# Fewer unread products in front, unread products between the sums of the norm, another price list for the order, and three late rows in flight in place of two

## The chip, the cores and the metric

The kernel runs on one core of one Trainium2 chip, as one program with one launch. The time is the device time of one execution in microseconds (us), and the figure for a kernel is the median over several executions.

## The reference

One layer of a diffusion backbone over 512 latent tokens and 256 context tokens, width 1024, all in float32:

```python
mod   = silu(c) @ w_ada + b_ada          # 6 vectors of 1024: shift, scale, gate, twice
mod_c = silu(c_ctx) @ w_ada + b_ada
h  = rms_norm(x, g_norm1) * (1 + sc1) + sh1
hc = rms_norm(ctx, g_norm1) * (1 + csc1) + csh1
aq, ak, av, dq, dk, dv, dz, da, db, ga, gd = split_cols(h @ w_in)      # the same for hc
y_attn = window_ctx_attention(q_a, k_a, v_a, k_ac, v_ac, attn_sink)    # 8 heads, window 128
o_dc, s_cf, s_cb = bidir_delta(context ...)      # gated delta rule, chunks of 64, both directions
o_dl, _, _       = bidir_delta(latent ..., s_cf, s_cb)
y = sigmoid(ga) * (y_attn @ w_br_attn) + sigmoid(gd) * (y_d @ w_br_dn)
x_new = x + gt1 * (y @ w_out)
x_new = x_new + gt2 * (square(relu(hm @ w_mlp1)) @ w_mlp2)   # hm: second norm, with sh2, sc2
```

## The kernel before

Activations lie transposed, features on the 128 partitions and tokens along the free dimension. A float32 product that must be exact is made of three products of rounded float32 (`mm3`: upper by upper, upper by lower, lower by upper; lines 331, 333 and 335). A product of plain float32 shows in the trace as two matmul instructions.

**The front.** Constants are set, `NONES` products of `ones` by `ones` (line 230) run on TensorE, and nobody reads them. The DMA queue of SyncE (SP) loads x, the context and sixteen halves of the first two sixths of `w_ada`. `norm_x` squares x in four pieces (ScalarE, line 402), folds each piece (VectorE, line 405) and sums over the partitions with one plain float32 product per piece (line 406); `Ln` and `Exp` make the factor `rx`. `ada(kt)` (line 249) and `columns(kt, ...)` (lines 267 to 282) make scale and shift of one block of 128 features; `features(kt)` (lines 339 to 341) makes the normalized, modulated block, and `early_x` and `early_c` multiply it with three early weight tiles. Two more groups of unread products stand in the front: eight after the first `columns` (line 276, `NWAIT`) and eleven more behind later ones (line 434, `WARM`). All other products of the layer follow these.

**The late modulation.** The other four sixths of `w_ada` are no matmuls: `late_mod` loads 32 rows of 512 KB each and sums each on VectorE (line 511). The load of a row waits for the sum of the row `NROWS` before it:

```python
d = nc.sync.dma_start(out=wa.ap, in_=I["wada2"][grp, j])
if len(sums) >= NROWS:
    tie(d.ins, sums[-NROWS], sync)
r = V.scalar_tensor_tensor(wa.ap, wa.ap, 0.5, scr_[0].ap, ...)
```

The first 16 of them stand beside the stage in which the delta rule's inverse is combined (`combine`, lines 993 to 1017), the intra-chunk matrices are made (`half_products`, line 894; lines 1395 to 1408) and the latent scan begins (`chain_step`, small products, line 1243). Products of the branch and gate projections fill TensorE there (`run_fill`, line 1148).

**The order.** The program is written once in a plain order. Then `arrange` gives every engine and the SP queue one fixed order: `Lists.run` is a list scheduler. It keeps a clock for TensorE, VectorE, ScalarE, GpSimd and SP, has a price for every instruction (`Step.cost`, how long it holds its engine and when its result is there), and takes on each engine the ready instruction with the lowest rank. The rank is the place in the written order, moved by `SHIFTS`: entries (engine or -1 for all, first place, end place, how many places to move). So a changed price or shift changes no instruction, only the order in which an engine takes them. DMA issues have their place in the SP order in the same way.

Of the kernel before, what the change touches and what calls it, by code (L numbers as in the profile page):

```python
# [26 lines left out]
LEAD = 0  # L27
ATT = 32
NHALF = 3
NONES, NWAIT = 30, 8  # L30
AHEAD = 2
LATES = 3, 3
HPAUSE = 2
# [3 lines left out]
STICK = 50  # L37
NSKIP = 2
WARM = (0, 3, 3, 3, 2, 0, 0, 0)
NROWS = 2  # L40
ND1 = 3
NGD = 5
P = 128
# [8 lines left out]
HC = CH // 2  # L52
# [65 lines left out]
def tile_layer(ctx: ExitStack, tc: tile.TileContext, I: dict, out: bass.AP, dbg=None):  # L118
    nc = tc.nc
    V, A, G, PE = nc.vector, nc.scalar, nc.gpsimd, nc.tensor  # L120
# [17 lines left out]
    banks = Arena(lambda o, n: psum[:, o:o + n], 512, 8)  # L138
# [55 lines left out]
    ones = mats.tile([P, P], F32, name="ones")  # L194
# [33 lines left out]
    wb_ = banks.get(512, True)  # L228
# [166 lines left out]

    def norm_x():
        ss = bank()
        for i in range(4):
            b = alloc(1024)
            src = xs_[:, i * 1024:(i + 1) * 1024]  # L400
            n = 512 if i == 3 else 1024
            A.activation(b[:, :n], src[:, :n], AF.Square)
            if i == 3:
                V.tensor_tensor(b[:, n:], src[:, n:], src[:, n:], op=ALU.mult)
            V.tensor_tensor(b[:, :512], b[:, :512], b[:, 512:], op=ALU.add)
            PE.matmul(ss.ap, ones, b[:, :512], start=(i == 0), stop=(i == 3))
            b.free()
        act(rx, ss.ap, AF.Ln, bias=epsc, scale=1.0 / D)
        ss.free()
        return act(rx, rx, AF.Exp, scale=-0.5)  # L410
# [177 lines left out]
    own = [slice(0, 64), slice(64, 128)]  # L588
# [1163 lines left out]
class Step:  # L1752
# [39 lines left out]
    def cost(self):  # L1792

        n = self.cols
        if self.kind == "InstMatmult":
            if self.dtype.endswith("32r"):
                return (226 if n == 512 else max(60, 7 + .44 * n)), n * .44 + 175
            if self.dtype.endswith("16"):
                return 96, 240
            if self.whole:  # L1800
                return (110, 280) if self.ins.is_transpose else (max(62, 1.72 * n), max(62, 1.72 * n) + 170)
            return (142, 300) if self.tile[0] == P else (30 if self.tile[1] > HC else 19, 220)
        if self.kind == "InstStreamTranspose":
            return 1950, 2090
        if self.eng == "DVE":
            own = 67 + 1.04 * n + 60 * self.psum if n > 8 else 100
            return own, own + 85
        if self.eng == "Activation":
            own = 1290 if "Load" in self.kind else max(195, 36 + .893 * n) + 20 * self.psum
            return own, own + 130  # L1810
        return 550, 560
# [69 lines left out]
class Lists:  # L1881
# [27 lines left out]
    def run(self, rank):  # L1909

        n, after, gang, eng = self.n, self.after, self.gang, self.eng
        left, ready = list(self.left), [0.] * len(self.left)
        wait = [len(m) for m in self.members]
        free, links = [0., 0., 0., 0., 750.], [0., 0., 0., 0., 3200.]
        coming, here, out = [[] for _ in free], [[] for _ in free], []
        flight, whole, cold = [], True, False
        words, asked, begun, last = 0, {n: 0. for n in range(3)}, [0.] * n, 0.
        push, pop = heapq.heappush, heapq.heappop
        note = [SEEN[e] for e in self.ENGINES]

        def go(k):
            if k >= n:
                for x in after[k]:
                    ready[x] = max(ready[x], ready[k])
                    left[x] -= 1
                    if not left[x]:
                        go(x)
            elif gang[k] is None:
                push(coming[eng[k]], (ready[k], rank[k], k))
            else:  # L1930
                g = gang[k]
                wait[g] -= 1
                if not wait[g]:
                    t = max(ready[x] for x in self.members[g])
                    for x in self.members[g]:
                        push(coming[0], (t, rank[self.members[g][0]], x))

        for k in [k for k, m in enumerate(left) if not m]:
            go(k)
        for _ in range(n):  # L1940
            t, e = min((free[e] if here[e] else max(free[e], coming[e][0][0]), e) for e in range(5) if here[e] or coming[e])
            mine, come = here[e], coming[e]
            while come and come[0][0] <= t:
                push(mine, pop(come)[1:])
            k = mine[0][1]
            if e == 0 and self.whole[k] != whole:
                same = min((x for x in mine if self.whole[x[1]] == whole), default=None)
                if same and same[0] <= mine[0][0] + STICK:
                    k = same[1]
                    mine.remove(same)  # L1950
                    heapq.heapify(mine)
                else:
                    pop(mine)
            else:
                pop(mine)
            out.append(k)
            if self.dma[k]:
                if e == 4:
                    if len(flight) >= 8:
                        t = max(t, flight[-8])  # L1960
                    links[e] = end = max(t + (2400 if self.bytes[k] > 100000 else 1600), links[e]) + self.bytes[k] / 422
                    flight.append(end)
                    free[e] = t + 400
                else:
                    links[e] = end = max(t + 2400, links[e]) + self.bytes[k] / 159
                    free[e] = t + 900
            else:
                own, lag = self.cost[k]
                if e == 0:
                    words, had = words + self.words[k], words  # L1970
                    block = int(words / 256 + .63)
                    if block > int(had / 256 + .63):
                        asked[block] = max(t + 1100, links[4] - 500) + 1250
                    t = max(t, asked.get(int(had / 256 - .54), 0))
                    if self.whole[k] != whole:
                        t += 92 if whole else 130
                        cold = whole = self.whole[k]
                    elif cold and whole and self.wide[k]:
                        t, cold = t + 100, False
                end = t + lag  # L1980
                free[e] = t + own
            begun[k], last = t, max(last, end)
            for x in after[k]:
                if x >= n:
                    at = end + 40
                elif eng[x] == e and not self.dma[k]:
                    at = free[e] if e == 0 else end + 10
                else:
                    at = end + note[eng[x]]
                if at > ready[x]:  # L1990
                    ready[x] = at
                left[x] -= 1
                if not left[x]:
                    go(x)
        return out, begun, last


SHIFTS = (
# [12 lines left out]
)  # L2011


# [120 lines left out]
```

## Time and profile before

| | us |
|---|---|
| median of 3 executions | 871.31 |
| lowest and highest | 870.93, 871.32 |
| the profiled execution: its time | 871.5 |
| its span in the profile | 869.7 |

The span runs from the first instruction to the last; 1.8 us of the profiled execution lie around it. PE is TensorE's matmuls, PEld its weight loads, DVE is VectorE, ACT is ScalarE, POOL is GpSimd, SPq the DMA issues of SyncE. A matmul's end is modelled and reaches into the next one, so the sum of durations of a group is more than the time that it takes. "L406" is line 406 of the kernel before.

### The profile page before, as it was taken

To read this page: it belongs to the slowest core of one execution; us is meant where nothing else is said; L and a number is where in the kernel's file an instruction comes from. 1 tells how busy PE (TensorE), PEld (TensorE's weight loads), DVE (VectorE), ACT (ScalarE), POOL (GpSimd) and SP (SyncE) were. 2 spreads that over 40 slices of the span, in tenths; PEclk is the share of its full clock that TensorE was granted. 3 is DMA by queue.
4 is the path that set the end of the run, shared out by engine and by line. 5 is a ranking of instruction groups with operands and counts; after the bars stand their busy time and mean duration, and the time that the engine had idled before them with its cause. 6 is when DMAs were issued, how large, how long until landed. Compare 5 with 4: busy or idle time off the path is not lost.

```text
span 869.7 us, 17973 instructions
## 1 busy us (share of the span) xinstructions
PE 852.3 (98%) x7544; PEld 712.8 (82%) x7544; DVE 647.0 (74%) x1113; ACT 498.4 (57%) x882; POOL 26.1 (3%) x42
## 2 busy tenths in 40 slices
PE   9999999999999999899999999999999999999998
PEld 6688778877777778677778899888998899889986
DVE  4865899987779997867848969993876478648741
ACT  5567875487669886587754435552555256415620
POOL 0000001010000002000000000000000000000000
PEclk9999999999999999999999999999999999999999
DMA  9924465533121236733116744743412332342031
GB/s 365 352 72 98 88 134 122 120 76 70 38 38 31 68 131 212 243 99 100 40 54 220 264 144 131 249 139 121 146 33 74 122 140 70 97 128 92 26 121 49
DMA packets 31986, 106.86 MB, mean 123 GB/s; under 512 B 4001, under 2 KB 4513, under 8 KB 31905
## 3 DMA queue, kind: packets, MB, share of 16 engines
q1 hardware_dynamic: 29600, 97.33, 33.6%
q0 software_dynamic: 2304, 8.39, 6.2%
q8 instruction: 59, 0.97, 0.5%
q14 instruction: 23, 0.18, 0.1%
HBM read 103.61 MB, written 2.10 MB: 122 GB/s over the span
## 4 chain that ended last, share of the span: by engine, by line
PE 77%; DVE 9%; ACT 6%; DMA 6%; issue 2%; SPq 0%; ACTq 0%; DVEq 0%
PE banks L331 14%; PE banks L333 14%; PE banks L335 14%; PE banks L1612 14%; PE banks L1148 7%; DMA m<-in_wada 3%; PE banks L1243 3%; PE banks L1194 3%; ACT m L185 2%; PE banks L725 1%; DVE wl L300 1%; DMA wr<-in_win 1%; PE banks L781 1%; DVE m L511 1%; DMA wr<-in_wbr 1%
## 5 line engine op out<-in xcount | busy, mean ns | idle before, releaser
L331 PE MATMUL banks<-m,wh 128*128 128x512 f32 (+1 forms) x568 | 210.7, 374 | 2.2 <-ACT m L224 1.3
L333 PE MATMUL banks<-m,wh 128*128 128x512 f32 (+1 forms) x568 | 211.2, 372 | 0.0
L335 PE MATMUL banks<-m,wl 128*128 128x512 f32 (+1 forms) x568 | 209.9, 370 | 0.1
L295 ACT ACTIVATE wh<-wr 128x1024 fp32r<-128x1024 f32 (+1 forms) x92 | 90.4, 984 | 128.3 <-PE banks L333 82.7
L331 PEld LDWEIGHTS banks<-m,wh 128*128 128x128 f32 x568 | 107.0, 189 | 20.4 <-ACT m L224 1.5
L1612 PEld LDWEIGHTS banks<-m,m 128*128 128x128 f32 x1008 | 122.2, 192 | 0.7
L335 PEld LDWEIGHTS banks<-m,wl 128*128 128x128 f32 x568 | 106.9, 188 | 19.2 <-issue 1.0
L1612 PE MATMUL banks<-m,m 128*128 128x256 f32 x1008 | 122.4, 283 | 0.0
L333 PEld LDWEIGHTS banks<-m,wh 128*128 128x128 f32 x568 | 107.1, 188 | 18.1 <-issue 0.7
L224 ACT ACTIVATE m<-m 128x512 fp32r<-128x512 f32 (+2 forms) x118 | 82.4, 721 | 66.1 <-PE banks L1612 14.9
L1148 PE MATMUL banks<-m,wh 128*128 128x512 f32 x320 | 104.1, 402 | 1.8 <-ACT m L185 1.0
L225 DVE TENSOR_TENSOR m<-m,m 128x512 fp32r<-128x512 f32 (+2 forms) x118 | 92.3, 804 | 15.5 <-ACT m L224 13.9
L300 DVE TENSOR_TENSOR wl<-wr,wh 128x1024 fp32r<-128x1024 f32 (+1 forms) x76 | 84.3, 1109 | 17.1 <-ACT wh L295 14.6
L1739 DVE SCALAR_TENSOR_TENSOR m<-banks,modT,m 128x512 f32<-128x512 f32 x32 | 24.0, 749 | 65.0 <-PE banks L335 64.9
L1148 PEld LDWEIGHTS banks<-m,wh 128*128 128x128 f32 x320 | 58.6, 188 | 14.4 <-ACT m L185 1.4
L1148 PE MATMUL banks<-m,wl 128*128 128x512 f32 x160 | 63.7, 400 | 0.4 <-DVE wl L300 0.4
L331 PE MATMUL banks<-m,m 128*128 128x256 f32 (+1 forms) x136 | 45.5, 340 | 0.4 <-ACT m L295 0.3
L333 PE MATMUL banks<-m,m 128*128 128x256 f32 (+1 forms) x136 | 45.6, 342 | 0.1
L511 DVE SCALAR_TENSOR_TENSOR m<-m,m 128x1024 f32<-128x1024 f32 x32 | 39.1, 1222 | 8.4 <-DMA m<-in_wada 8.2
L335 PE MATMUL banks<-m,m 128*128 128x256 f32 (+1 forms) x120 | 40.2, 337 | 0.0
L1243 PEld LDWEIGHTS banks<-m,m 64*64 64x64 f32 x1600 | 26.7, 134 | 12.5 <-issue 4.3
L1148 PEld LDWEIGHTS banks<-m,wl 128*128 128x128 f32 x160 | 30.0, 188 | 7.3 <-DVE wl L300 1.1
(263 smaller groups left out, 1313.7 us busy)
## 6 DMA issues: line engine op xcount, KB each, us to landing
m<-in_wada SPq DMA_DIRECT2D x48, 512.0 KB, 4.8
wr<-in_wm SPq DMA_DIRECT2D x40, 512.0 KB, 3.6
wr<-in_win SPq DMA_DIRECT2D x38, 512.0 KB, 3.7
m<-in_wm SPq DMA_DIRECT2D x24, 512.0 KB, 3.7
wl<-in_win POOLq DMA_DIRECT2D x16, 512.0 KB, 5.8
m<-in_xT SPq DMA_DIRECT2D x8, 512.0 KB, 5.9
wr<-in_wbr SPq DMA_DIRECT2D x16, 256.0 KB, 2.7
wr<-in_wout SPq DMA_DIRECT2D x8, 512.0 KB, 4.4
```

The lines of the kernel that those rows point to most:

```text
L224: A.activation(r32(hi), src, AF.Copy)
L225: (eng or V).tensor_tensor(r32(lo), src, hi, op=ALU.subtract)
L295: upper[0] = A.activation(r32(hi), raw, AF.Copy)
L300: V.tensor_tensor(r32(lo), raw, hi, op=ALU.subtract)
L331: PE.matmul(acc, w[0][:, k, :], xhi, start=(start and i == 0), stop=False)
L333: r = PE.matmul(acc, w[0][:, k, :], xlo, start=False, stop=(end and w[1] is None))
L335: r = PE.matmul(acc, w[1][:, k, :], xhi, start=False, stop=end)
L511: r = V.scalar_tensor_tensor(wa.ap, wa.ap, 0.5, scr_[0].ap, op0=ALU.mult, op1=ALU.mult, accum_out=modT[:, grp, j:j + 1])
L1148: PE.matmul(acc.ap, w[x][:, k, :], hx[k][y], start=(k == p == 0), stop=(k == KT - 1 and p == 2))
L1194: PE.matmul(pa.ap, w[x][:, j, :], r32(Q[y][:, :, j, :]), start=(j == p == 0), stop=(j == 3 and p == 2))
L1243: runs[n].append(PE.matmul(out_, w, x, start=True, stop=True).ins.name)
L1612: PE.matmul(dst, r32(self.w[w][i][:, k * P:(k + 1) * P]), xs7[x][k][j], start=(n == 0), stop=(n == 11))
```

## The change

Six things are edited. `NONES` goes from 30 to 16. In `norm_x`, 0, 4, 2 and 0 unread products of `ones` by `ones` follow the four products of line 406 (`XWARM`), in one more PSUM bank that is free again afterwards. `NROWS` goes from 2 to 3. The price list gets other numbers: a 16-bit product 80 in place of 96, a plain float32 product at least 224 and 1.33 per column in place of 1.72 per column, a product of 128 rows on fewer columns of the array 108 with its result after 400, in place of 142 and 300. In the list's clock, TensorE's prices are doubled before 5500 ns (`COLD`). A DMA that follows another DMA of the same queue only by an order tie need no longer wait in the list for the first one to land. All 60 entries of `SHIFTS` are replaced by 58 others; there are 8 products fewer in the program, so places count otherwise too.

```diff
-NONES, NWAIT = 30, 8
+NONES, NWAIT = 16, 8
...
-NROWS = 2
+XWARM = (0, 4, 2, 0)
+COLD = 5500
+NROWS = 3
...
     def norm_x():
         ss = bank()
+        wb_ = banks.get(512, True)
         for i in range(4):
...
-            PE.matmul(ss.ap, ones, b[:, :512], start=(i == 0), stop=(i == 3))
+            pe = PE.matmul(ss.ap, ones, b[:, :512], start=(i == 0), stop=(i == 3))
             b.free()
+            for _ in range(XWARM[i]):
+                follow(PE.matmul(wb_[:, :P], ones, ones, start=True, stop=True), pe)
+        wb_.free()
...
             if self.dtype.endswith("16"):
-                return 96, 240
+                return 80, 240
+            if self.whole and not self.ins.is_transpose:
+                return (max(224, 1.33 * n), max(224, 1.72 * n) + 170)
             if self.whole:
-                return (110, 280) if self.ins.is_transpose else (max(62, 1.72 * n), max(62, 1.72 * n) + 170)
-            return (142, 300) if self.tile[0] == P else (30 if self.tile[1] > HC else 19, 220)
+                return 110, 280
+            return (108, 400) if self.tile[0] == P else (30 if self.tile[1] > HC else 19, 220)
...
                 if e == 0:
+                    if t < COLD:
+                        own, lag = 2 * own, lag + own
...
                 elif eng[x] == e and not self.dma[k]:
                     at = free[e] if e == 0 else end + 10
+                elif eng[x] == e and self.dma[x]:
+                    at = free[e]
...
 SHIFTS = (
-    (0, 2729, 2759, -37), (0, 7350, 8025, -10), (-1, 4917, 4924, 10), (0, 1436, 2436, 180), (-1, 5117, 5177, 30),
...
+    (0, 1428, 2428, 360), (-1, 2012, 2032, 120), (0, 7639, 7699, 80), (0, 1540, 1940, -30), (-1, 1584, 1604, -120),
...
```

## Rows read from the trace of the kernel before

**Rows 1.** The page's first lines: span, busy time and share by engine.

```profile
span 869.7 us, 17973 instructions
PE 852.3 (98%) x7544; PEld 712.8 (82%) x7544; DVE 647.0 (74%) x1113; ACT 498.4 (57%) x882; POOL 26.1 (3%) x42
```

**Rows 2.** Five stretches: length, busy time (instructions) by engine, clock, DMA share, GB/s.

```profile
0.00:42.00 42.00, 39.10 (x306) 28.12 (x310) 27.34 (x64) 24.57 (x41) 1.68 (x6) 1.00 0.95 370
42.00:330.00 288.00, 282.78 (x2448) 225.71 (x2440) 242.13 (x449) 211.66 (x380) 16.07 (x20) 1.00 0.37 85
330.00:382.00 52.00, 48.43 (x1083) 38.66 (x1083) 39.69 (x67) 33.95 (x64) 8.32 (x16) 1.00 0.54 185
382.00:480.00 98.00, 96.21 (x1411) 75.47 (x1412) 72.64 (x147) 60.32 (x175) 0.00 (x0) 1.00 0.35 109
480.00:866.00 386.00, 385.79 (x2305) 344.80 (x2303) 264.48 (x391) 167.89 (x226) 0.00 (x0) 1.00 0.37 120
```

**Rows 3.** PE's waits, 330 to 382 us: releaser, us, times, longest.

```profile
PE banks L1004 <- issue: 1.2, 1, 1.2
PE banks L894 <- DVE m L1398: 0.8, 1, 0.8
PE banks L1148 <- ACT wh L295: 0.8, 1, 0.8
PE banks L1243 <- ACT m L1282: 0.8, 1, 0.8
```

**Rows 4.** Stretches of the unread products of line 230 alone: PE, PEld, clock, DMA.

```profile
2.00:3.00 1.00, 1.00 (x7) 1.00 (x6) 1.00 0.71 238
...
2.00:4.00 2.00, 2.00 (x11) 2.00 (x10) 1.00 0.87 320
...
6.00:7.00 1.00, 1.00 (x12) 1.00 (x11) 1.00 1.01 401
...
6.00:8.00 2.00, 2.00 (x21) 2.00 (x20) 1.00 1.01 404
```

**Rows 5.** Timeline of the front, 0 to 22 us: start, duration, engine, line.

```profile
1.06 8.43 PE L230 MATMUL banks<-ones 128*128 128x128 f32 x60 [1.06 <-DVE ones L195]
...
5.49 0.69 DVE L405 TENSOR_TENSOR m<-m 128x512 f32<-128x512 f32 x1 [4.18 <-ACT m L402]
...
6.73 0.69 DVE L405 TENSOR_TENSOR m<-m 128x512 f32<-128x512 f32 x1 [0.54 <-ACT m L402]
...
8.73 0.69 DVE L405 TENSOR_TENSOR m<-m 128x512 f32<-128x512 f32 x1 [1.31 <-ACT m L402]
...
9.33 3.60 PE L406 MATMUL banks<-m,ones 128*128 128x512 f32 x8
...
10.13 0.69 DVE L405 TENSOR_TENSOR m<-m 128x512 f32<-128x512 f32 x1
...
11.86 1.28 ACT L181 ACT_TABLE_LOAD   x1
...
12.86 1.07 PE L249 MATMUL banks<-m,m 128*32 128x256 f32 x16
...
13.69 0.67 ACT L185 ACTIVATE m<-banks,epsc 128x512 f32<-128x512 f32 x1
...
14.68 0.61 PE L272 MATMUL banks<-c_prm,m 128*128 128x2 f32 x4 [0.76 <-ACT m L267]
...
21.06 0.64 PE L249 MATMUL banks<-m,m 128*32 128x256 f32 x8 [0.15 <-DMA m<-in_wada]
```

**Rows 6.** Stretches of the front: PE, PEld, DVE, ACT, POOL, clock, DMA share, GB/s.

```profile
20.00:25.00 5.00, 4.54 (x34) 2.46 (x32) 3.17 (x9) 2.62 (x4) 0.00 (x0) 1.00 1.02 419
25.00:30.00 5.00, 4.91 (x46) 3.22 (x48) 4.94 (x12) 2.51 (x7) 0.00 (x0) 1.00 1.02 419
30.00:35.00 5.00, 4.73 (x52) 2.98 (x41) 3.95 (x9) 3.12 (x7) 0.73 (x1) 1.00 1.02 417
```

**Rows 7.** The loads of the late rows, 300 to 400 us, and what waits.

```profile
DVE m L511: 7.8, 8
...
DMA to landing us min/median/max: 3.5/4.4/5.4
```

**Rows 8.** Chain of waits, 320 to 382 us, in order of time: start, us, what.

```profile
337.87 4.46 DMA m<-in_wada
...
342.42 1.25 DVE m L511 x2
...
343.68 4.27 DMA m<-in_wada
```

**Rows 9.** Stretch from 340 to 360 us: busy time by engine, clock, DMA.

```profile
340.00:360.00 20.00, 18.82 (x517) 15.36 (x520) 14.02 (x23) 9.92 (x16) 4.16 (x8) 1.00 0.76 258
```

22 rows, old and new, of the table SHIFTS are left out of this document.

## The prediction, made before the changed kernel ran

> **What bounds the kernel now.** First the page's shares: TensorE is busy for 98% of the span, VectorE for 74%, ScalarE for 57% [rows 1]. So only an edit that takes away time in which TensorE stands still, or makes it stand more, can move the end. Where does it stand? The stretches answer that, as length less busy time [rows 2]: 2.9 us before 42 us, 5.2 from 42 to 330, 3.6 from 330 to 382, 1.8 from 382 to 480, and 0.2 in all of the 386 us up to 866. With 3.7 us behind the last product that is the page's difference of 17.4 us. The reader should see two things in this. The second half is closed: no order and no faster load gains anything there. And what the change can win is small, some 13 us if every wait went. The clock column stands at 1.00 in every stretch, so no stretch of some length is at the lower of TensorE's two levels; the first microseconds need the pace of the products instead (below).
>
> Then each stretch by what releases TensorE. From 330 to 382 us the waits are four: one on TensorE's own issue (1.2), three behind VectorE and ScalarE (0.8 each) [rows 3]. In the front the DMA engines are full (share 1.02 at 417 to 419 GB/s from 20 to 35 us) and VectorE is next, 4.94 of 5 us from 25 to 30 [rows 6].
>
> **The front: 14 unread products less.** A window counts what reaches into it, so the pace is the longer window less the shorter one: 4 in the added microsecond at 2 to 4 us, 9 at 6 to 8 [rows 4]. The level doubles in between, from 1.2 to 2.4 GHz, although the clock column says 1.00 in both. With 0.22 us for one at first and 0.111 later, 60 instructions from 1.06 to 9.33 [rows 5] need the turn at about 4.3 us: 15 before it, 45 behind it. Sixteen products are 32 instructions: 15 up to 4.3 and 17 more, 1.9 us, to 6.2. The first fold of the norm ends at 5.49 + 0.69 = 6.18 [rows 5], so the products end when the first read one can begin, and no hole opens. At present that product waits until 9.33.
>
> The read ones take 3.60 us for four, 0.9 each. Now the last fold (10.13 + 0.69 = 10.82) sets the last of them: it ends at 11.7 in place of 12.93, 1.2 us earlier [rows 5]. What follows gets less: the table load ends at 13.14, so `Ln` can begin at most 0.55 us before its present 13.69 [rows 5]. At 21.06 the third block waits for its DMA half, which no edit moves [rows 5]. What can be kept is work that VectorE does before its full stretch from 25 us on [rows 6]. So the gain lies between 0 and 1.2 us; I take 0.6, near the `Ln` row, because that is the next thing released.
>
> **Six products between the sums.** They are 12 instructions at 0.111, 1.3 us. Four follow the second read product: the second fold ends at 7.42, the product at 8.3, the four at 9.2, before the third fold ends at 9.42. Two follow the third: from 10.3 to 10.8, and the last fold ends at 10.82 [rows 5]. The wait for VectorE hides them, so they cost nothing; without that cover they would cost at most 1.3 us. The extra bank is free again before the projections.
>
> **Does the clock hold?** The rows show that it rose while products ran without a hole from 1.06 on, and stayed up through the holes of the front, such as 0.76 us at 14.68 [rows 4, 5]. The changed front has holes of 0.2 to 0.4 us. By these rows it costs nothing. The Trainium skill, "TensorE: Matmul & The Clock Gate", section "Part 1: The HAM clock gate", says that the rise is bought with busy time and not with a number of products, and that its moment varies from run to run; by that rule too short a run-up could leave the front at the lower level, the clock rival below. The trace agrees with the first half (a rise in the midst of equal products); that the moment varies no run here shows yet.
>
> **Three late rows in flight.** A row lands 4.4 us after its issue (median) [rows 7], its sum takes 1.25, and the chain shows just this pair in turn [rows 8]. With two in flight a row comes every (4.4 + 1.25) / 2 = 2.8 us, with three every 1.9. Twelve rows lie in 333 to 366 us, so they could be done some 11 us sooner; VectorE stands before them for 7.8 us in all [rows 7]. VectorE takes its work in order: behind a waiting sum stand the folds for the intra-chunk matrices (lines 1395 to 1398) and the weights' lower halves (line 300), and for those wait ScalarE's copies and then the three TensorE waits behind VectorE and ScalarE [rows 3]. Those are the most that can be won, 2.4 us; the issue wait is no matter of VectorE. The DMA engines, at a share of 0.76 from 340 to 360 us [rows 9], have room for the same bytes somewhat sooner. Below lies 0 (the waits are not due to the rows), and a loss if weights come later (a rival). I take 1.7 of 2.4, since all three sit at 367 to 380 us, right behind the row chain. The other 16 rows come after 466 us, where TensorE hardly waits: 0.
>
> **The new prices and shifts.** No instruction changes, only orders, and so the other waits: 5.2 us in 42 to 330 and 1.8 in 382 to 480, 7.0 in all [rows 2]. The bounds are 7.0 won and, for an order that fits worse, as much again lost. Some prices come nearer to the rows: two two-column products take 0.61 us (line 272), the list had 0.12 and now has 0.45; the front's first products run at half pace to 4.3 us, which the list did not know. Others go off: a product of line 406 takes 0.9 us, the list had 0.88 and now has 0.68; eight products of line 249 take 1.07 us, 134 ns each, had 142, now 108 [rows 5]. So neither direction is clear from prices; I take a sixth of the 7.0 as won, 1.2, nearer to nothing than to either end.
>
> **Sum.** 871.5 (the profiled execution) - 0.6 - 1.7 - 1.2 = 868.0. That execution lies 0.2 above the median of 871.31, so 867.8 for a median. All gains at their bounds would give 871.3 - 1.2 - 2.4 - 7.0 = 860.7.
>
> **Rivals.** *Nothing moves.* The front's 1.2 us vanish behind the full DMA engines, and the fill products already cover the rows; for it speaks the DMA wait at 21.06 [rows 5], against it the DVE waits of 7.8 us [rows 7]. 871.
>
> *The new order fits worse.* One place is enough: 42 to 330 us, where attention and inverse interleave on VectorE (242 of 288 us busy) and ScalarE (212) [rows 2]. If VectorE takes inverse steps ahead of what a score or a projection waits for, the 5.2 us double: 871.3 + 5.2 = 876.5. It decides once that idle time exceeds 9 us, more than the other two terms give back. For it: two prices went off. Against: two came nearer.
>
> *Weights behind rows.* The third row stands in front of a weight load of 512 KB in the same queue; at 258 GB/s [rows 9] each would land 2.0 us later. Some weights already come just in time: TensorE waits 0.8 us for a split at line 295 [rows 3]. With two such in the stretch, less what the rows win: 871.3 + 4.0 - 1.7 = about 874. Against: a row load that waits for a sum also holds up the weights behind it, and that wait gets shorter.
>
> *The clock.* The run-up of 5.1 us in place of 8.3 does not hold the upper level. One fall of the length at the start (3.2 us) costs 1.6 us; half pace up to 35 us costs up to 15, since TensorE is busy 14.2 of the 15 us from 20 on [rows 6]. Midway: 871.3 + 8 = about 879. This is what the rule of the page on the clock gate would do here.
>
> **Chances.** Forecast (faster, 862 to 869.5): 0.62. Nothing moves: 0.14. Order worse: 0.13. Weights behind rows: 0.05. Clock: 0.06. The three executions lie within 0.4 us, so about 0.2% (1.7 us) is what can be told from no change: faster 0.62, same 0.14, slower 0.24. The likeliest case alone spans 863 to 869.5. The range from 862 to 876 leaves out the gains near all bounds (0.08) and the clock and the worst orders (0.10).
>
> **What would show it.** Line 230 with 32 instructions ending near 6.2 us at pace 9 in its last microsecond; line 406 beginning at 6.2 and ending near 11.7; `Ln` near 13.2. Sums of line 511 every 2 us instead of 2.8, and their DMA wait (7.8 us) mostly gone; TensorE's idle time in 330 to 382 us falling from 3.6 to about 2, in 42 to 330 from 5.2 to about 4.2. The prediction is wrong if idle time between 42 and 480 us grows, if weight splits wait for their DMA beside the rows, or if equal products in the front keep the half pace.

## The result, and the profile after

The changed kernel takes 874.29 us (median of 7 executions, 872.23 to 875.52), the kernel before beside it 871.32 (7 executions, 870.93 to 872.71). The ratio is 1.003, with a 95% interval of 1.0018 to 1.0041: slower by 0.3%, where the prediction said 0.4% faster. The time lies inside the range of 862 to 876, but that is no credit to the sum: the range was wide enough to hold rivals that the forecast spoke against.

The profiled execution is the fastest of the seven, 872.23, with TensorE's granted clock at 1.00 throughout. It is only 0.7 us above the profiled one of before. One more, 872.87, had the clock at 1.00; the other five had a mean granted clock of 0.993 to 0.997 and took 873.86 to 875.52. So two things have to be explained: 0.7 us that the profile shows, and some 2 us that go together with a lower clock.

First the page of the kernel after, to be held against [rows 1]:

```profile
span 870.4 us, 17943 instructions
PE 850.6 (98%) x7528; PEld 713.2 (82%) x7528; DVE 649.1 (75%) x1113; ACT 498.2 (57%) x882; POOL 26.0 (3%) x42
```

TensorE works 1.7 us less, on 16 matmul instructions fewer, and the span is longer all the same: TensorE stands still 2.4 us more. The same five stretches as in [rows 2] say where (length, busy time by engine, granted clock, DMA share, GB/s):

```profile
0.00:42.00 42.00, 38.43 (x289) 27.11 (x293) 26.41 (x63) 22.43 (x37) 1.70 (x6) 1.00 0.94 363
42.00:330.00 288.00, 281.77 (x2419) 226.12 (x2412) 241.38 (x445) 212.50 (x384) 16.04 (x20) 1.00 0.36 83
330.00:382.00 52.00, 47.23 (x1022) 37.98 (x1024) 42.03 (x69) 32.70 (x60) 8.29 (x16) 1.00 0.60 202
382.00:480.00 98.00, 96.73 (x1505) 76.54 (x1506) 72.28 (x145) 62.12 (x177) 0.00 (x0) 1.00 0.34 109
480.00:866.00 386.00, 385.88 (x2308) 345.27 (x2307) 266.21 (x393) 168.42 (x226) 0.00 (x0) 1.00 0.36 120
```

Idle time, length less busy time, is 3.6, 6.2, 4.8, 1.3 and 0.1 us, where it was 2.9, 5.2, 3.6, 1.8 and 0.2. From 42 to 480 us it is 12.3 in place of 10.6; that it grows there was one of the prediction's own signs of being wrong. The stretch from 330 to 382 us, where the prediction wanted 1.6 us less, has 1.2 more. VectorE is busy for 42.03 us there, before 39.69. What released TensorE in it (compare [rows 3]):

```profile
PE banks L900 <- DVE m L1404: 2.1, 1, 2.1
PE banks L900 <- issue: 1.5, 1, 1.5
PE banks L999 <- issue: 1.1, 1, 1.1
```

L900 and L1404 are lines 894 and 1398 of before: `half_products` and the last fold that it reads. That wait was 0.8 us and is 2.1, and a second one of 1.5 follows in the same group of products. The late rows (compare [rows 7]):

```profile
L514 SPq DMA_DIRECT2D m<-in_wada x15: 327/328/600, 327.4 to 391.5; - x15
...
  DVE m L517: 4.4, 6
...
DMA to landing us min/median/max: 3.5/5.0/7.4
```

Here the step went the way that was foretold, though not as far (the wait was to be mostly gone): VectorE waits 4.4 us for rows instead of 7.8, although a row lands 0.6 us later in the median. That was worth nothing, and VectorE's and TensorE's timelines show why (start, duration, engine, line):

```profile
336.25 1.21 DVE L517 SCALAR_TENSOR_TENSOR m<-m,m 128x1024 f32<-128x1024 f32 x1
...
361.92 1.23 DVE L517 SCALAR_TENSOR_TENSOR m<-m,m 128x1024 f32<-128x1024 f32 x1 [0.56 <-DMA m<-in_wada]
...
364.28 0.41 DVE L1401 TENSOR_TENSOR m<-m,banks 128x256 f32<-128x256 f32 x1
...
367.45 1.22 DVE L517 SCALAR_TENSOR_TENSOR m<-m,m 128x1024 f32<-128x1024 f32 x1
...
368.69 0.87 DVE L1403 TENSOR_TENSOR m<-m,banks 64x256 f32<-64x256 f32 x2
369.58 0.69 DVE L1404 TENSOR_TENSOR m<-m,banks 128x512 f32<-128x512 f32 x1
```

```profile
367.75 0.44 PE L1249 MATMUL banks<-m,m 64*64 64x64 f32 x10
370.33 1.10 PE L900 MATMUL banks<-m,m 64*32 64x64 f32 x88 [2.14 <-DVE m L1404]
371.36 0.69 PE L1249 MATMUL banks<-m,m 64*64 64x64 f32 x32
371.99 0.53 PE L900 MATMUL banks<-m,m 64*32 64x64 f32 x22
374.04 0.43 PE L900 MATMUL banks<-m,m 64*32 64x64 f32 x18 [1.52 <-issue]
374.40 0.73 PE L1154 MATMUL banks<-m,wh 128*128 128x512 f32 x2
```

Twelve sums from 336.25 to 361.92 are one every 2.3 us, before one every 2.9 (332.86 to 365.26). But the series begins 3.4 us later, the last three of the twelve now run ahead of the first fold at 364.28, and the new order puts a thirteenth sum, at 367.45, ahead of the last fold. In the kernel before that one comes behind it, at 372.54. VectorE works without a gap of 0.1 us from 361.92 to the end of the last fold at 370.27. TensorE had run out at 368.19. In the kernel before the last folds of the group and TensorE beside them run like this:

```profile
366.50 0.42 DVE L1395 TENSOR_TENSOR m<-m,banks 128x256 f32<-128x256 f32 x1
...
368.97 0.68 DVE L1398 TENSOR_TENSOR m<-m,banks 128x512 f32<-128x512 f32 x1
```

```profile
366.92 0.44 PE L1243 MATMUL banks<-m,m 64*64 64x64 f32 x10
368.13 0.73 PE L1148 MATMUL banks<-m,wh 128*128 128x512 f32 x2 [0.78 <-ACT wh L295]
369.70 1.48 PE L894 MATMUL banks<-m,m 64*32 64x64 f32 x128 [0.84 <-DVE m L1398]
371.12 0.73 PE L1148 MATMUL banks<-m,wh 128*128 128x512 f32 x2
```

No sum stands among these last folds (two, at 363.00 and 365.26, stand before them), the last one ends at 369.65, and TensorE has projection products of `run_fill` just before and just after `half_products`. In the kernel after, those come only at 374.40.

Starts of the same product, at places where both kernels have issued the same work, give the lag of the new kernel: +0.6 us at 65 us, 0.0 at 255, +0.8 at 367 (the ten small products at 366.92 before and 367.75 after), +3.0 at 379, +1.4 at 470, +0.3 at 554 and +0.7 at the end. So most of the 3.0 us is lost at the folds, and what follows the late stage wins 2.7 back from 379 to 554 us, before another 0.4 goes. In the front the products of line 230 (L232 now), the last two unread ones of `XWARM` (L412) and the read ones (L409) stand thus (compare [rows 5]):

```profile
1.06 6.78 PE L232 MATMUL banks<-ones 128*128 128x128 f32 x32 [1.06 <-DVE ones L197]
7.68 1.02 PE L409 MATMUL banks<-m,ones 128*128 128x512 f32 x2
...
11.93 0.61 PE L412 MATMUL banks<-ones 128*128 128x128 f32 x4
12.37 1.02 PE L409 MATMUL banks<-m,ones 128*128 128x512 f32 x2
```

The 32 instructions take 0.21 us each, half pace for nearly the whole run-up, and the last sum of the norm begins at 12.37 where 10.82 was foretold. The pace is not what makes it late. The new order issues two small loads of constants ahead of x, as the SP queue shows, after and then before:

```profile
0.75 0.39 SPq L150 DMA_DIRECT2D c_cc<-in_cc  x1
...
1.66 1.85 SPq L262 DMA_DIRECT2D m<-in_xT  x4
```

```profile
0.75 1.81 SPq L260 DMA_DIRECT2D m<-in_xT  x4
```

So the first square begins at 5.42 instead of 4.41, and the last fold ends here, at 12.00 instead of 10.82:

```profile
11.31 0.69 DVE L408 TENSOR_TENSOR m<-m 128x512 f32<-128x512 f32 x1
```

The other 0.4 us up to 12.37 are unread products (line 412), which TensorE still runs when that fold is done.

### The profile page after: what moved, and what is told of

Read it like the earlier page. It is cut to its first block, busy times and chain, and to the rows that moved or that the text cites. A ratio compares the mean times of both kernels' runs of the same rounds, so it can differ in the third digit from the quotient of the medians.

```text
span 870.4 us, 17943 instructions
## 1 busy us (share of the span) xinstructions
PE 850.6 (98%) x7528; PEld 713.2 (82%) x7528; DVE 649.1 (75%) x1113; ACT 498.2 (57%) x882; POOL 26.0 (3%) x42
## 4 chain that ended last, share of the span: by engine, by line
PE 77%; DVE 9%; ACT 7%; DMA 5%; issue 2%; SPq 0%; DVEq 0%; ACTq 0%
PE banks L333 14%; PE banks L335 14%; PE banks L1618 14%; PE banks L337 14%; PE banks L1154 6%; DMA m<-in_wada 5%; PE banks L1249 3%; PE banks L1200 2%; ACT m L187 2%; PE banks L731 1%; PE banks L787 1%; DVE m L979 1%; DVE m L989 1%; PE banks L721 1%; DVE m L978 1%
## 5 line engine op out<-in xcount | busy, mean ns | idle before, releaser
L335 PE MATMUL banks<-m,m 128*128 128x256 f32 (+1 forms) x136 | 44.2, 341 | 0.2 <-DVE m L343 0.2
L333 PE MATMUL banks<-m,m 128*128 128x512 f32 (+1 forms) x136 | 43.7, 341 | 0.4 <-ACT m L342 0.3
L337 PE MATMUL banks<-m,m 128*128 128x512 f32 (+1 forms) x120 | 38.7, 334 | 0.0
```

The costliest lines, as they stand in the source:

```text
L333: PE.matmul(acc, w[0][:, k, :], xhi, start=(start and i == 0), stop=False)
L335: r = PE.matmul(acc, w[0][:, k, :], xlo, start=False, stop=(end and w[1] is None))
L337: r = PE.matmul(acc, w[1][:, k, :], xhi, start=False, stop=end)
```

## The experiments

The twelve were measured in three batches of four, each on one chip beside the kernel before, whose median there was 871.80 us, then 871.84, then 872.13; ratios are taken within a batch. "Order held" means that each engine keeps the order of its parent kernel, so that only the named edit differs.

**The front.** Was it the shorter run-up? a_none30 gives the changed kernel its 14 products back, b_none16 takes them from the kernel before; order held in both.

```diff
-NONES, NWAIT = 16, 8      # a_none30, on the changed kernel
+NONES, NWAIT = 30, 8
-NONES, NWAIT = 30, 8      # b_none16, on the kernel before
+NONES, NWAIT = 16, 8
```

> The changed kernel with 30 unread products in front again, every engine's order held as in the changed kernel. Theory 1 (clock): with 16 products the front falls back to the lower level for some microseconds in most executions, which makes the mean granted clock of five of the seven executions 0.993 to 0.997 and costs about 2 us; with 30 all executions show a mean clock of 1.000 and the median is 872 to 873, within 1 us of each other. Theory 2 (the order alone made it slower): clocks and median stay, 874 to 875.

> The kernel before with 16 unread products in front in place of 30, every engine's order held as in the kernel before, none between the sums. Theory 1 (clock): mean clocks under 1.000 in most executions and a median 1.5 to 3 us above the kernel before, 873 to 874. Theory 2: no difference, 870.5 to 872, since the products are not read and the order is the same.

a_none30 took 874.04 us, ratio 1.0022 (1.001 to 1.0034): the loss stays, so it isn't the run-up. b_none16 took 872.80, ratio 1.0012 (1.0001 to 1.0024): no gain from fewer products. That lies above the 870.5 to 872 of its second theory and below the 873 to 874 of its first. Its front shows the saving come and go:

```profile
1.07 6.74 PE L231 MATMUL banks<-ones 128*128 128x128 f32 x32 [1.07 <-DVE ones L196]
7.64 3.83 PE L407 MATMUL banks<-m,ones 128*128 128x512 f32 x8
```

The run-up has the same half pace as in the kernel after, yet the read products begin at 7.64 instead of 9.33 and are done at 11.47. `Ln` begins at 13.20, just where the prediction had it, but not by its path. In both kernels `Ln` stands on ScalarE right behind a copy (line 313; 13.15 before, 12.67 here), and the copy behind the table load; that chain begins when a load of constants lands, here at 11.14 instead of 11.62. The 0.5 us that `Ln` is ahead of before are down to 0.1 from 24.5 us on.

a_none30 also shows what the lower clock does. First the timeline with its one long wait of TensorE from 330 to 384 us, then the stretch at the lower level (columns as in the five stretches):

```profile
372.84 1.55 PE L901 MATMUL banks<-m,m 64*32 64x64 f32 x88 [3.60 <-DVE m L1405]
374.33 1.13 PE L1250 MATMUL banks<-m,m 64*64 64x64 f32 x32
```

```profile
371.90:378.70 6.80, 5.86 (x166) 4.92 (x167) 5.03 (x11) 6.59 (x13) 0.00 (x0) 0.50 0.01 2
```

The granted clock is 0.50, the level of 1.2 GHz, for 6.8 us; it fell at 371.9, in the last microsecond of the wait. The 32 small products take 1.13 us where the kernel after, at the upper level, takes 0.69 (371.36 above).

**The third row in flight, the order held.** b_rows3 lets the load wait for the sum three before, and nothing else.

```diff
-                tie(d.ins, sums[-NROWS], sync)
+                ties.append((d.ins.name, sums[-NROWS]))          # for the list: 2, as before
+            if len(sums) >= FLIGHT:                               # for the chip: 3
+                tc.add_manual_dep(d.ins, sums[-FLIGHT], sync, reason="order")
```

> The kernel before with three late rows in flight, every engine's order held. If VectorE's waits for the rows are what TensorE waits for at 367 to 380 us: 1 to 2.4 us faster, 869 to 870.3. If TensorE's waits there come from the order of the work and not from the rows: 871 to 872, with VectorE's wait for rows down from 7.8 us to under 4 and TensorE's idle time from 330 to 382 us still 3 to 4 us.

871.27 us, ratio 0.999 (0.9981 to 1.0). By that ratio the third row in itself wins 0.9 us, with an interval from 0 to 1.7, and loses nothing. But the first reading's ground, a wait of VectorE under 4 us, is not there. With the order held VectorE still waits 7.4 us for rows from 330 to 384 us, and the SP queue shows at least part of why. Its row loads wait less for sums (5.3 us from 320 to 380 us in place of 16.4), but they stand in one queue with weight loads that wait for VectorE's lower halves, and that wait grows: here 19.6 us, in the kernel before 13.4.

```profile
DVE m L513 <- DMA m<-in_wada: 7.4, 6, 2.8
```

```profile
SPq L290 <- DVE wl L300: 19.6, 7, 5.6
```

```profile
SPq L290 <- DVE wl L300: 13.4, 7, 6.1
```

**Orders joined.** Each of the next four kernels has its orders written out by engine, put together at places where both orders have issued the same work.

```diff
-    for k in settled(Lists(steps, needs(steps, ties), gangs)):
+    for k in held(len(steps)):
```

mix30: 30 products in front, three rows in flight only after the sixteenth; before's order to 65 us, the changed one from 65 to 259, before's to 435, the changed one to 554, before's to the end.

> The orders of both kernels, cut where both have issued the same work: the kernel before up to 65 us, the changed one's from 65 to 259, the kernel before's from 259 to 435, the changed one's from 435 to 554, the kernel before's from there; 30 products in front, rows two in flight for the first sixteen and three after. By the lags between the two profiles (-0.7, -1.6 and -1.1 us in the stretches taken from the changed kernel) 868 to 868.5 with all clocks 1.000. If the gains of those stretches were given by what lay before them (a late start that is caught up), 870 to 871.5.

868.50 us (6 executions, 867.71 to 868.90), ratio 0.9958 (0.9942 to 0.9973): faster than both kernels by 3 us and more. The new order does win something in two of its stretches, and 259 to 379 us, where it lost 3.0 us, is the suspect. That was tried from both sides: a_midb is the changed kernel with before's order in 259 to 379 us, b_mida the kernel before with the changed order there and three rows in flight.

> The changed kernel with the order of the kernel before in one stretch, from 259 to 379 us (both have issued the same work at either end), three rows in flight. Theory 3 (late stage): the new order of that stretch loses 3.0 us to holes of TensorE and lets its clock fall there in most executions, 1 to 2 us more; here 870 to 871.5 and mean clocks of 1.000 in most executions. Rival (the falls and the loss come from elsewhere, such as the later front): 873 to 875 with the falls kept.

> The kernel before with the changed kernel's order in the stretch from 259 to 379 us and three rows in flight, 30 products in front. Theory 3: 3 to 5 us above the kernel before, 874 to 876.5, the clock below its upper level for 3 to 7 us near 370 us. Rival: 870.5 to 872, as with three rows in flight alone.

a_midb: 870.26 us, ratio 0.9985 (0.9976 to 0.9993). b_mida: 872.69, ratio 1.0011 (1.0001 to 1.002). So giving back this stretch turns the changed kernel from 0.3% slower to 0.15% faster. With the granted clock at 1.00 in both, the profiled spans are 868.2 us and 870.4. In the kernel before the same order costs only 0.1%, 0.9 us where 3 to 5 were expected: what the stretch costs depends on what stands around it, and why it is so much less there stays open. The wait for the last fold goes with the order; TensorE's waits of a_midb from 330 to 384 us have

```profile
PE banks L903 <- DVE m L1407: 0.3, 1, 0.3
```

and those of b_mida have, at the same fold,

```profile
PE banks L897 <- DVE m L1401: 2.7, 1, 2.7
```

a_frontb gives the changed kernel before's order up to 65 us.

> The changed kernel with the order of the kernel before up to 65 us: x and the first w_ada half go ahead of the two small constant loads again; 16 products in front and six between the sums as in the changed kernel. If the small loads in front cost their place: the first square begins near 4.4 us in place of 5.42, the lag of 0.6 us at 65 us is gone or turns into a gain of up to 0.7, median 873 to 873.8. If the front hides it: 874 to 874.6.

873.71 us, ratio 1.002 (1.001 to 1.003): within the interval of the changed kernel. In its profile the first square begins at 4.53 us, and it is 1.4 us ahead of the kernel after at 65 us, still 1.2 at 335. It has lost that by 345, where its granted clock is 0.50 for 3.4 us.

**VectorE's time or the transfers?** a_thin is the changed kernel, order held, with all loads and shorter sums: it leaves out 960 of the 1024 columns in each of the first sixteen.

```diff
+            c = slice(0, 64 if len(sums) < 16 else 1024)
-            r = V.scalar_tensor_tensor(wa.ap, wa.ap, 0.5, scr_[0].ap, ...)
+            r = V.scalar_tensor_tensor(wa[:, c], wa[:, c], 0.5, scr_[0][:, c], ...)
```

> The changed kernel, order held, in which the first sixteen late rows are loaded whole but only 64 of their 1024 columns are summed (work left out), so that a row takes VectorE 0.2 us in place of 1.22. If VectorE's time is what TensorE waits for at 367 to 378 us: the wait of 2.1 us before line 900 goes, 870 to 871.5, few falls of the clock. If it is the rows' transfer or the place in the order: 873.5 to 875.

870.54 us, ratio 0.9995 (0.998 to 1.0011): the loss is gone though every byte still moves. (Nine of its eleven executions took 869.76 to 872.27, two 875.38 and 875.91.) The sum among the folds takes 0.22 us, the last fold begins at 367.61 instead of 369.58, and TensorE's wait for it is 0.4 us, as VectorE's timeline and TensorE's waits show:

```profile
366.47 0.22 DVE L521 SCALAR_TENSOR_TENSOR m<-m,m 128x64 f32<-128x64 f32 x1
...
367.61 0.69 DVE L1408 TENSOR_TENSOR m<-m,banks 128x512 f32<-128x512 f32 x1
```

```profile
PE banks L904 <- DVE m L1408: 0.4, 1, 0.4
```

The second wait in the same group stays, at 1.3 us. This kernel has some 16 us less of VectorE's work in all, and the kernel before with such sums was not run; how much of the 3 us it would win as well is not shown.

**Which edit of the list?** The last four were measured together: mix30 with three rows in flight for all 32 rows, and the kernel before with one edit of the list at a time, its order worked out anew.

```diff
-            flight = 2 if len(sums) < 16 else 3                   # mix_rows3, on mix30
-            if len(sums) >= flight:
-                tie(d.ins, sums[-flight], sync)
+            if len(sums) >= NROWS:
+                tie(d.ins, sums[-NROWS], sync)
...
-NROWS = 2                                                         # b_nrows3, on the kernel before
+NROWS = 3
...
-                return 96, 240                                    # b_price: the four prices of a product
+                return 80, 240
...
-    (0, 2729, 2759, -37), (0, 7350, 8025, -10), ...               # b_shifts: all entries
+    (0, 1428, 2428, 360), (-1, 2012, 2032, 120), ...
```

> The kernel with both orders joined, three late rows in flight for all 32 rows in place of two for the first sixteen; order held. If the time that VectorE spends on the rows is what counts, and not how soon a row lands, the time stays that of the joined kernel, 868.5, give or take 0.5. If rows that land sooner pay, as the prediction had it, it falls by up to 1.7 us, to 866.8. If three rows crowd out weights, it rises to 870 or more.

> The kernel before with three rows in flight, and the list told of it, so that the order is worked out anew; prices and places stay. If it is the third row in the list that puts the row sums ahead of the folds, TensorE stands behind line 1398 for 2 us or more from 365 to 380 us and the time is 873 to 874.5. If the prices and places do that, the order hardly changes and the time is 870.5 to 871.5, as with three rows in flight and the order held (0.999).

> The kernel before with the changed kernel's prices of a product alone; the order is worked out anew, places stay. If the prices alone put the sums ahead of the folds, the time is 873 to 874.5 with TensorE behind line 1398 for 2 us or more. If they describe the chip better and the places were the fault, it is 868.5 to 870.5. If old places just do not fit new prices, idle time of TensorE is spread over 42 to 480 us and the time is over 874.5.

> The kernel before with the changed kernel's entries of SHIFTS (places counted with 8 products fewer), old prices, two rows; the order is worked out anew. If the entries alone put the row sums ahead of the folds, the rows start some 4 us later and TensorE stands behind line 1398 for 2 us or more: 873 to 874.5. If it takes the new prices too, the sums keep their place and what remains is new places on old prices: anything from 869.5 to 880, with the idle time elsewhere than at line 1398.

| kernel | median us (executions) | ratio to before, 95% interval |
|---|---|---|
| mix_rows3 | 868.29 (5) | 0.9956 (0.9944 to 0.9969) |
| b_nrows3 | 873.43 (10) | 1.0018 (1.0009 to 1.0028) |
| b_price | 883.77 (4) | 1.0135 (1.0117 to 1.0153) |
| b_shifts | 891.29 (4) | 1.0224 (1.021 to 1.0238) |

mix_rows3 cannot be told from mix30 (the intervals are 1.1 to 1.4 us to either side): with the order held, the first sixteen rows gain nothing that shows from a third one in flight. VectorE's wait for them hardly falls there, from 8.7 us to 7.9. b_nrows3 is the telling one. Telling the list of three rows costs 1.3 us on 872.13, where the same three rows with the order held cost nothing. VectorE's wait for rows is down to 0.6 us, and it now has a sum at 367.52 among the folds, as in the changed kernel:

```profile
367.52 1.22 DVE L511 SCALAR_TENSOR_TENSOR m<-m,m 128x1024 f32<-128x1024 f32 x1
...
369.66 0.69 DVE L1398 TENSOR_TENSOR m<-m,banks 128x512 f32<-128x512 f32 x1
```

Half of its expectation missed: in the profiled execution, its slowest (875.79), TensorE does not wait at that fold, because projection products cover it until then. Its waits from 330 to 382 us are others, 2.5 us at line 1004 (before 1.2) and 2.0 behind line 1282 (before 0.8), and at the end of the first and right behind the second the clock falls to the lower level, as the two stretches show:

```profile
PE banks L1004 <- issue: 2.5, 1, 2.5
PE banks L1243 <- ACT m L1282: 2.0, 1, 2.0
```

```profile
351.90:355.20 3.30, 3.26 (x44) 2.72 (x45) 2.44 (x4) 2.35 (x4) 1.04 (x2) 0.50 0.62 220
382.60:386.00 3.40, 3.40 (x76) 2.99 (x66) 2.91 (x5) 2.76 (x10) 0.00 (x0) 0.50 0.48 149
```

b_price and b_shifts say that neither half of the new list stands alone: they cost 12 and 19 us with the rest of the list old. b_shifts lies above all that was expected of it (880 at most). In both a sum also stands right ahead of the last fold, at 373.55 and 377.19, with two rows in flight: so the third row is enough to put it there, but not the only edit that does. Moving only the late rows' sums behind the folds was not tried: later work waits for the buffers that those rows use.

## Why the prediction was wrong

**The step that failed** is the pair of late rows and new order. The prediction gave the rows 1.7 us from the stretch of 330 to 382 us, as if VectorE's order there stayed, and gave the new order only the waits of the other stretches ("5.2 us in 42 to 330 and 1.8 in 382 to 480"). But a third row changes a tie that the list reads, and so do prices and places, so the order in the rows' own stretch is new too. There it was a loss: 3.0 us of lag between 255 and 379 us, and TensorE's wait for the last fold 2.1 us where it was to shrink from 0.8. a_midb, which changes only that order, takes the loss away; a_thin, which takes VectorE's time out of it, does too; b_nrows3 shows that the third row in the list alone makes such an order and costs 0.2%. b_mida shows the wait, but only 0.9 us of loss.

**Rows in flight.** The sums did come faster (2.3 us instead of 2.9) and VectorE waited 3.4 us less for rows. But that came with the new order. With the order held, as the prediction had it, the wait hardly goes (7.4 of 7.8 us in b_rows3), where the row loads stand behind weight loads in their queue. What is left is worth 0.9 us by b_rows3 (interval 0 to 1.7) and nothing that shows by mix_rows3; the 1.7 of the sum was the upper end. So there were two mistakes: to take the sum before it as all that a row load waits for, and to count the wait that goes and not the 1.2 us of VectorE that each sum takes, ready or not. A sum that is ready earlier is only useful if nothing behind it in VectorE's order is urgent.

**New prices and shifts.** Taken at -1.2. With the old order in 259 to 379 us the whole change is worth -1.3 us (0.15% in a_midb), front and rows included, and the best joined order -3.3 to -3.8. So the sign was right there and the size near. But 1.2 was a sixth of a bound and not worked out from any wait, so that it is near is luck, and the bounds of 7.0 each way held only for prices and places that belong together; alone they lose 12 and 19 us.

**Front.** Taken at -0.6. Fewer products alone measure +1.0 us (0.1 to 2.1, b_none16). With the order held `Ln` does come 0.5 us earlier, by luck, since the prediction overlooked the copy that stands before it; and 0.1 us of that is left at 24.5 us. The rival in which the gain vanishes was right for this term. The changed kernel doesn't even have the 0.5: the prediction took the folds at their old places, while the new order loads x later, and `Ln` comes at 13.75, behind the copy again (13.22), which waits for its load. The lag of 0.6 us at 65 us goes with that order (a_frontb is 1.4 us ahead there), but a_frontb's time does not tell it from nothing. What the front's lag costs at the end stays open. The six products between the sums were put at nothing; the last of them hold the sum back by up to 0.4 us.

**The rivals.** "The new order fits worse" was right in kind and too large (876.5), with its place wrong: 42 to 330 us grew by 1.0 us of idle time, 330 to 382 by 1.2 and with falls of the clock. "Weights behind rows" did not happen: no wait on a split weight is among TensorE's three waits in that stretch after. "The clock" was right that a lower level could cost time, and right that the front would stay longer at half pace, but wrong that the loss comes from there: a_none30 has the long run-up and the same loss. Where a profile shows the lower level after the front, it is at the late stage's waits (b_shifts has two such stretches more, at other waits).

**How the 3 us come about.** In the profiled execution 2.4 us of idle time less 1.7 us of work leave 0.7. The median is 2.1 us above that execution, and five of seven executions had a lower mean clock. That those executions lost it behind the wait for the last fold is likely, since a_none30 has the same order and shows it there; for the changed kernel itself no profile of such an execution exists.

## What to carry to other kernels

A new dependence in a list-scheduled kernel is two changes, what the chip waits for and the order that the list makes of it; hold the order and change the dependence alone, then let the list run, and the two prices come apart (0.999 and 1.0018 here). The order is also that of the loads in their queue: a load freed of one wait can stand behind another that waits (7.4 of 7.8 us were left in b_rows3). On an engine that takes its work in order, price a transfer that comes earlier by what its consumer then pushes back, not by the wait that goes. When two orders of the same program win in different stretches, joining them at places where both have issued the same work is worth a try: here it gave a time 0.4% below that of the kernel before.

## What the hardware showed beside that

A wait in this kernel can cost more than its length. In the profiles above, stretches at half the granted clock began within a wait or at most 1.7 us behind one (waits of 1.5, 2.0, 2.5 and 3.6 us) and lasted 3.4 to 6.8 us. What ran in them took longer: in a_none30 the 88 small products take 1.55 us instead of 1.10 in the kernel after, the 32 take 1.13 instead of 0.69. Not every such wait has one: the profiled execution after has 2.1 and 1.5 us and stays at 1.00. On one chip mean clocks of 0.999 or less were seen in 14 of 29 executions of the kernel before, in 10 of 12 of a_none30 and in 1 of 6 of mix30; on another in 18 of 35, in 10 of 11 of b_mida and in 4 of 11 of a_midb. So it seems that the order changes how often it happens, though mix_rows3, with mix30's order, has 3 of 5 on a third chip. The Trainium skill, "TensorE: Matmul & The Clock Gate", section "HAM oscillation — how this bites in real kernels", tells of such falls where products wait for DMA between short groups; here they come at waits behind VectorE and ScalarE, too, in a stretch with a DMA share of 0.01 (a_none30's row above).

The rise at the start differs between executions of equal fronts: 60 instructions of line 230 took 8.43 us in the profile of before [rows 5] and 9.84 in that of b_nrows3 (the line below); 32 took 6.78 in that of the kernel after and 5.37 in that of a_frontb.

```profile
1.06 9.84 PE L230 MATMUL banks<-ones 128*128 128x128 f32 x60 [1.06 <-DVE ones L195]
```

The Trainium skill, "TensorE: Matmul & The Clock Gate", section "Part 1: The HAM clock gate", says that its moment varies from run to run, in its example by half a microsecond either way. The runs agree that it varies, and here two equal fronts differ by 1.4 us. Of these 0.2 us were left at 27.7 us, so a turn of the clock fitted from one profile, as the prediction did with 4.3 us, is a poor base for a sum.
